# New priority offsets for the planner that orders every engine of a one-core backbone step

## The chip, the core and the metric

The kernel runs on one core of one Trainium2 chip. Its time is the device time of one execution in microseconds (us), the median of the runs shown. The core has a matrix engine (TensorE, PE in the profile, with its weight loads as PEld), a vector engine (VectorE, DVE), a scalar engine (ScalarE, ACT), GpSimd (POOL) and a sync engine (SyncE, SP). Each works through a list of instructions of its own, in order; SP and POOL also issue the transfers (DMA).

## The reference, cut to what matters

One inference step of a diffusion backbone with one layer: 1024 latent tokens and 128 context tokens, width 1024, all in float32.

```python
def block(x, mod, s_hgrn, s_rwkv, ffn_conv_fn, p):
    shift1, scale1, gate1, shift2, scale2, gate2 = jnp.split(mod[:, None, :], 6, axis=-1)
    h = rmsnorm(x, p['norm_mix_w']) * (1 + scale1) + shift1
    u = h @ p['w_in']
    o_a, s_hgrn_new = hgrn2_mixer(u[..., :P_A], p['lb'], p['hgrn_norm_w'], s_hgrn)
    o_b, s_rwkv_new = rwkv7_mixer(u[..., P_A:], p, s_rwkv)
    x = x + gate1 * (jnp.concatenate([o_a, o_b], axis=-1) @ p['w_out'])
    h = rmsnorm(x, p['norm_ffn_w']) * (1 + scale2) + shift2
    gt = ffn_conv_fn(h @ p['ffn_w_gate']) + p['ffn_conv_b']
    x = x + gate2 * ((jax.nn.gelu(gt) * (h @ p['ffn_w_up'])) @ p['ffn_w_down'])
    return x, s_hgrn_new, s_rwkv_new
```

`mod` is a projection of the conditioning vector (`ada_w`, 1024 by 6144). `hgrn2_mixer` is a gated linear recurrence with 4 heads of 128, run forward and backward; `rwkv7_mixer` is a delta-rule recurrence with 8 heads of 64, run forward and backward; the FFN (2816 wide) has a 3x3 depthwise convolution on its gate branch. The context runs through the same block, a final norm follows, and the context's final states are returned too.

## The kernel before, in words

The kernel doesn't write its instructions in the order in which they run. `step_kernel` walks through the computation once and records every operation with a class `Plan`: what it reads and writes, on which engine it may run, and the source function that asked for it, its kind (for instance `chains`, `weights`, `product`). `Plan.schedule` then lays all operations out in time with estimated durations: whenever an engine is free, it takes the ready operation of the highest rank. `Plan.issue` emits them in that order, so each engine's list is fixed when the kernel is built. Semaphores then hold an instruction until what it needs is there; an engine never goes past an instruction that waits.

The rank is the longest remaining path behind the operation (`tail`) plus a `lead`, both in us of the planner's own estimates, with some corrections for the matrix engine's modes and the activation tables:

```python
op.place, op.dense, op.lead, op.kind = None, False, self.lead + LEADS.get(self.kind, 0.0) + self.nudge(self.kind), self.kind
...
        i = self.seen[kind] = self.seen.get(kind, -1) + 1
        x = NUDGE.get(kind, ())
        return x[i // 16] if i // 16 < len(x) else 0
...
                r = op.tail + op.lead
...
            x = max(cand, key=rank)
```

`NUDGE` has a list of offsets for each kind: the first holds for the first 16 operations of that kind in the order of recording, the second for the next 16, and so on, each between -200 and 200. An operation that may go to several engines (most copies to ACT or DVE, most stores to POOL or SP) goes to the one whose turn comes first, so a rank can also decide its engine. A tile of on-chip memory gets its place when its first operation is laid out.

In the order of time, the kernel's stages are these.

- Up to about 75 us: nine blocks of rows of x are loaded, normed and transposed (`turned`, L1208), the first third of `ada_w` is multiplied by the conditioning vector (`mod_columns`, L1252 and L1257), and the modulated rows are split into a high and a low float32r part (`hh`, `hl`).
- Up to about 500 us: the input projection. Each block of 128 columns of `w_in` is loaded (`wr`), split into `wh` and `wl`, and multiplied in three passes (`proj`, L1139 to L1141). `conv_rkv` and `features` make the RWKV operands (`pk`, L1474), `elim` inverts small triangular systems (L1539, L1541), `hgrn_in` (L1302) makes the HGRN2 operands (its transposes are L1315); all go to DRAM (`d_ak`, `d_kb`, `d_v`, `d_hq` and so on).
- About 500 to 960 us: two chains of 18 RWKV steps each (`chains`, L1808), with `hgrn_block`, `hgrn_out`, `bonus_rows` and the rest of `ada_w` (`ada_block`, L1031, matmuls at L1046) between them. A step loads `kb` (L1771) and `W` (L1773, from `d_ak`), then the values from `d_v`; `prep` multiplies the first two (L1790), and four small groups of matmuls follow (L1837, L1844, L1852, L1861 and L1863). `W` has one buffer for each of the two chains.
- About 900 to 1061 us: the output projection by blocks of 128 rows (`wo_tile`, L2033 to L2035), each after `post` has loaded `d_y` (L1937), normed it and transposed it (L1957), then transposes of the FFN's input (L2047).
- About 1037 to 1545 us: the FFN's gate and up projections, in 22 tiles of 128 columns. `weights` (L2102) loads quarters of the weights, two of them by accumulating transfers on POOL's queue, and `pair` splits them (L2115); `product` (L2137, matmuls at L2145) multiplies; `ffn_mid` does the convolution on DVE (L2234). `down_sums` (L2249) prepares sums of the down projection's weights with accumulating transfers into `d_t`.
- About 1545 us to the end: the down projection (`three`, L2310), with the last norm and the stores.

Of the kernel before, what the change touches and what calls it, by code (L numbers as in the profile page):

```python
# [44 lines left out]
HUNGRY = 2.04  # L45
BUSY = 168.59
ADDS = 2.1
NUDGE = {'step_kernel': [-74, -18, -9, 150, 12, -123, -45, 8, -171, -78, -136, -179, 107, -143, -58, 0, -130, -65, -5, 128, 32], 'const': [-22], 'turned': [97, -42, -193, -76, -114], 'param_loads': [-72, -193], 'params': [-93, -75], 'first_columns': [18, -146, -118, -43], 'mod_columns': [-171, 58, -11, -11], 'modulated': [79, 153, 129, 10, 26], 'conv_rkv': [-39, -180, -157, 76, -193, 38, -43, -113, -6, -198, -181, -15, -22, 19, -60, 38, 0, -14, -4, -2, -12, -36, -52, -68, -4, -22, -7, 16, 98], 'features': [11, 15, 5, 7, 7, 4, 12, 18, 19, 13, 4, -13, -25, 2, -15, -18, 15, 1, -1, 8, 135, 22, 13, -7, -9, 49, -12, 10, 52, -6, -13, 149, 113, -14, -42, 40, -39, 200, 53, 147, 194, 162, 146, 69, 156, 106, 12, 157, 6], 'hgrn_in': [-21, 125, -9, -10, -3, -22, 47, 74, -1, 110, 113, 101, 77, 73, 55, 34, 25, 33, 38, 3, -25, 85, 74, 33, -51, -81, 69, -27, -33, -47, -41, -43, -40, -39, 0, -60, -47, 104, -54, -124, -85, -102, -45, -44, -41, -135], 'elim': [-31, 11, 4, -66, 30, -24, -2, -54, 26, -8, 14, -1, -80, -6, 0, 9, 118, 94, 159, 130, -37, 65, 67, 117, 163, 18, -87, 0, 0, 123, -122, 147, 145], 'chains': [147, 1, 46, 57, 14, 65, 0, -12, 8, 8, 11, 13, -3, -1, -1, 8, 67, -31, 7, 6, 1, 3, -22, 31, 4, -52, 20, 12, 26, 5, 58, 9, 0, 2, 61, -1, 16, 119, 137, 172, 177, 46, 70, 24, 16, 4, -11, -33, -33], 'prep': [72, -66, -26, 76, -2, 6, 0, -48, -40, 7, -15, -126, 100, -34, -86, 10], 'bonus_rows': [-177, -200, 51, -33, -72, -25], 'ada_block': [-6, 0, -21, 2, 10, 48, 37, 5], 'hgrn_block': [-12, -21, 0, -11, -8, -40, -96, -124, -53, -1, 72, 69, 5, 18, -5, -20, -19, -3, 2, 200, 3, 8, -46, -18, -44, -41, -3, -19, -22, 30, -20, -4, 0, 0, -13, 1, 60, 55, 95, 184, -18, 10, 6, 62, 89, -33, 1, 26, 2, 81, 128, 59, -7], 'hgrn_out': [9, -29, 34, 20, -53, 0, 0, -4, -64, 73, -70, 6, 3, 17, 75], 'mod_scale': [-188], 'wo_tile': [74, -16, -30, 7, -28, -29, 44, -7, 150, 73, 184, 90, 92, 97, 131, 0, -123, 77, 96, 48, 9, 28], 'post': [-28, -2, 151, -25, 41, 199, 67, 74, 86], 'stored': [62], 'put': [126, 0, 132, 32, 194], 'made': [111, 72], 'weights': [-144, 9, -60, 11, 102, -11, -130, -37, -192, 175, 155], 'pair': [133, -65, 41, -35, 1, -6, -22, -48, -174, -122, -112, 86, 10, 2, -49, 4, -81, 8, -141, -112], 'product': [70, 200, 104, 27, 29, -16, -16, -184, -68, -45, -132, -1, -164, -66, 41, 99, 16, -86, -25, -3, -14, -152, -70, -36, -54, -54, -93, 1, -120, -6, -172, -200, -200, -186, -91, -200, -200, -200, -200, -126, -200, -146, -155, 0, -4, 141, -88, -81, -17, -88, 127, 198, -96, -15, 92, -90, -194, -157, -102, 45, -194, -107, -185, -153, -160, 0, -26, -195, -33, -76, 56, -171, -19, -134, -23, -47, -50], 'save': [80, 75, 47, -69, -200, -35, -175, -91, -12], 'front': [-40, 75, -32, -36, -46, -20, -166, -162, 5, 15, -150, -134, -86, -150], 'ffn_mid': [-11, -35, -68, -65, -37, -17, -131, -39, -113, -200, -152, -200, -173, -60, -61, -92, -181, -170, -125, -98, -94, -42, -41, -6], 'down_sums': [-86, -18, -200, 128, 29, 15], 'rows_of_context': [12, -134], 'tokens': [-1, -10, -25, -182, -89], 'part': [6, -6, -2, -5, -5, -75, -113, -24, -27, 32, 111, 198, 153, 116, 3, 5, -41, -72, 105, -10, -77, -95], 'weight': [175, 0, 196], 'three': [-41, 113, 9, 55, -48, -18, 9, -30, -23, 25, -93, 0, -67, -24, -19, -60, -81, 0, 88, 128, -28, -21, -38], 'gate_row': [75], 'kept': [-40], 'gated': [-59, -47, 14, 62], 'normed': [-200, 0, -37], 'put_out': [-72, -6], 'total': [-53, 29, 69]}
LEADS = {'ada_block': 46.4, 'bonus_rows': 27.8, 'chains': -35.7, 'const': 113.0, 'conv_rkv': 0.0, 'down_weights': -36.2, 'elim': -4.6, 'features': 0.0, 'ffn_down': 14.5, 'ffn_mid': -1.7, 'finish': 52.5, 'finish_last': -12.3, 'first_columns': -38.6, 'front': 0.0, 'gate_row': 0.0, 'hgrn_block': -3.6, 'hgrn_in': 0.0, 'hgrn_out': 113.5, 'late': -0.7, 'made': 3.5, 'mod_columns': -1.2, 'mod_scale': 70.4, 'modulated': -24.2, 'pair': 8.2, 'param_loads': 9.6, 'params': -96.8, 'post': 3.0, 'prep': 119.5, 'product': -3.4, 'put': 0.0, 'save': 4.8, 'step_kernel': -1.0, 'stored': 0.0, 'three': -10.1, 'total': -0.3, 'turned': 4.0, 'weights': 0.0, 'wo_tile': 5.1}


# [126 lines left out]
class Plan:  # L178
# [213 lines left out]
    def nudge(self, kind):  # L392
# [4 lines that stand above are left out]
# [2086 lines left out]
```

## Time and profile before

| | |
|---|---|
| Median of 3 runs | 1804.65 us (1803.7 to 1806.81) |
| The profiled execution's own time | 1804.31 us |
| Its span, first to last instruction | 1802.5 us |
| Mean granted clock of TensorE | 0.990 |
| Instructions | 44849 |
| Moved by DMA | 352.98 MB, on the mean 196 GB/s |

In the lines of the profile, an engine's time is followed by its share of the span and the number of its instructions; a line such as L2145 is the line of the kernel that asked for the operation. A wait is written as the engine, tile and line that waited, then what ended the wait ("issue" where the profile shows nothing that did). Matmuls overlap each other, so a busy PE has work in flight and may still be slowed. PEclk is the share of TensorE's full clock that was granted. The chain of waits is followed back from the last instruction.

### The profile page before, as it was taken

How to read it: one execution, taken by the hardware profiler on the slowest of the kernel's cores; microseconds unless marked ns; L12 is line 12 of the kernel's file. 1: busy time of each engine (PE TensorE's matmuls, PEld its weight loads, DVE VectorE, ACT ScalarE, POOL GpSimd, SP SyncE). 2: the span in 40 equal slices, each digit the busy share in tenths (PEclk: the TensorE clock that was granted, in tenths of full speed). 3: DMA queues.
4: the chain of work that ended last, by engine and by line, in shares of the span. 5: the costliest groups of instructions: out<-in, count | busy, mean ns of one | idle time of the engine just before them, and what ended most of it. 6: DMA issues, size and time to landing. Idle time of an engine off the chain costs nothing.

```text
span 1802.5 us, 44849 instructions
## 1 busy us (share of the span) xinstructions
PE 1731.0 (96%) x17726; PEld 1551.9 (86%) x17726; DVE 1455.2 (81%) x2793; ACT 936.1 (52%) x1921; POOL 441.7 (25%) x701
## 2 busy tenths in 40 slices
PE   6999999999999999999998989999999999999998
PEld 4888888888978788887777889999999999788886
DVE  7558998977778878886868877998879889868875
ACT  6556756542256545663635754444444444665542
POOL 2114335353322222223211112233332323100000
PEclk9999999999999999999999999999999999999999
DMA  9226547486676668888967657688877767997674
GB/s 325 95 64 173 127 122 177 109 216 188 199 211 205 203 207 280 280 273 263 320 185 258 227 117 146 128 184 169 161 151 154 158 143 164 282 341 230 195 254 146
DMA packets 321930, 352.98 MB, mean 196 GB/s; under 512 B 67771, under 2 KB 240217, under 8 KB 321368
## 3 DMA queue, kind: packets, MB, share of 16 engines
q1 hardware_dynamic: 255528, 245.56, 45.7%
q0 software_dynamic: 66192, 104.57, 25.1%
q8 instruction: 139, 2.28, 0.5%
q14 instruction: 71, 0.58, 0.1%
HBM read 254.99 MB, written 118.10 MB: 207 GB/s over the span
## 4 chain that ended last, share of the span: by engine, by line
PE 82%; DVE 7%; DMA 6%; issue 2%; ACT 2%; SPq 0%; POOL 0%; DVEq 0%; POOLq 0%; ACTq 0%
PE banks L2145 25%; PE banks L2310 14%; PE banks L1139 7%; PE banks L1141 6%; PE banks L1140 6%; PE banks L1790 2%; DMA fx<-d_y 1%; PE banks L2033 1%; PE banks L2034 1%; PE banks L2035 1%; PE banks L1837 1%; PE banks L1659 1%; PE banks L1844 1%; PE banks L1861 1%; DMA d_kb<-top 1%
## 5 line engine op out<-in xcount | busy, mean ns | idle before, releaser
L1139 PE MATMUL banks<-hh,wh 128*128 128x384 f32 x768 | 282.0, 367 | 1.4 <-DVE fx L1327 1.4
L1140 PE MATMUL banks<-hl,wh 128*128 128x384 f32 x768 | 259.9, 338 | 0.0
L1141 PE MATMUL banks<-hh,wl 128*128 128x384 f32 x768 | 259.9, 338 | 0.0
L2234 DVE SCALAR_TENSOR_TENSOR low<-low,pf 128x1024 f32<-128x1024 f32 x176 | 225.0, 1280 | 9.5 <-ACT low L2228 6.9
L2145 PE MATMUL banks<-qm,wh 128*128 128x320 f32 x968 | 224.8, 312 | 2.6 <-ACT wh L2115 2.4
L2145 PE MATMUL banks<-qm,wl 128*128 128x320 f32 x528 | 164.1, 311 | 2.9 <-DVE wl L2115 2.9
L2145 PE MATMUL banks<-hbm,wh 128*128 128x256 f32 x880 | 164.1, 284 | 2.0 <-DVE low L2013 1.5
L2145 PEld LDWEIGHTS banks<-qm,wh 128*128 128x128 f32 x968 | 162.0, 190 | 3.3 <-ACT wh L2115 2.7
L1139 PEld LDWEIGHTS banks<-hh,wh 128*128 128x128 f32 x768 | 146.0, 190 | 21.7 <-issue 13.4
L1140 PEld LDWEIGHTS banks<-hl,wh 128*128 128x128 f32 x768 | 146.5, 191 | 2.1 <-issue 1.4
L1141 PEld LDWEIGHTS banks<-hh,wl 128*128 128x128 f32 x768 | 146.0, 190 | 0.0
L2145 PEld LDWEIGHTS banks<-hbm,wh 128*128 128x128 f32 x880 | 139.8, 191 | 3.2 <-DVE low L2013 1.8
L2145 PE MATMUL banks<-ham,wh 128*128 128x256 f32 (+1 forms) x616 | 131.7, 294 | 0.0
L2183 ACT COPY fx<-banks 128x256 f32<-128x256 f32 (+1 forms) x132 | 52.3, 398 | 143.5 <-PE banks L2145 142.4
L2145 PE MATMUL banks<-hbm,wl 128*128 128x256 f32 x440 | 124.8, 284 | 0.0
L2145 PEld LDWEIGHTS banks<-qm,wl 128*128 128x128 f32 x528 | 99.7, 189 | 4.2 <-DVE wl L2115 4.2
L2145 PEld LDWEIGHTS banks<-ham,wh 128*128 128x128 f32 x616 | 102.0, 190 | 0.1
L2115 ACT CAST wh<-low 128x512 fp32r<-128x512 f32 x88 | 54.4, 619 | 57.7 <-DMA low<-in_ffn_w_up_dram 32.4
L2145 PEld LDWEIGHTS banks<-hbm,wl 128*128 128x128 f32 x440 | 84.3, 192 | 0.0
L2145 PE MATMUL banks<-ham,wl 128*128 128x256 f32 (+1 forms) x264 | 77.1, 292 | 0.0
L2115 DVE TENSOR_TENSOR wl<-low,wh 128x512 fp32r<-128x512 f32 x88 | 60.3, 687 | 16.5 <-ACT wh L2115 16.1
L2254 POOL DMA_DIRECT2D d_t<-in_ffn_w_down_dram x44 | 43.0, 1093 | 86.5 <-DMA d_t<-d_t 42.2
(604 smaller groups left out, 4442.9 us busy)
## 6 DMA issues: line engine op xcount, KB each, us to landing
wr<-in_w_in_dram SPq DMA_DIRECT2D x34, 512.0 KB, 4.1
d_t<-in_ffn_w_down_dram POOLq DMA_DIRECT2D x57, 256.0 KB, 5.4
low<-d_a SPq DMA_DIRECT2D x54, 256.0 KB, 4.7
low<-d_ak SPq DMA_DIRECT2D x64, 192.0 KB, 4.4
low<-in_ffn_w_gate_dram SPq DMA_DIRECT2D x44, 256.0 KB, 3.5
low<-in_ffn_w_up_dram POOLq DMA_DIRECT2D x44, 256.0 KB, 5.5
low<-d_kb SPq DMA_DIRECT2D x36, 256.0 KB, 3.9
d_a<-low POOLq DMA_DIRECT2D x16, 576.0 KB, 4.4
```

The costliest lines, as they stand in the source:

```text
L1139: mm(o, wh[:, kt, :], hh[:, kt, c], kt == 0, False)
L1140: mm(o, wh[:, kt, :], hl[:, kt, c], False, False)
L1141: mm(o, wl[:, kt, :], hh[:, kt, c], False, kt == KT - 1)
L1659: mm(pv[r, i, :], xs[:, t0:t0 + 32], view(qy, t0, [[2 * m, 16 // m], [B + m, 2], [1, m]]), True, True)
L1790: mm(pa[h][:, P * w:P * w + P], kb[hc[h], w, :], W[hc[h], A0[h] + 192 * w:A0[h] + 192 * w + P], True, True)
L1837: mm(R[hc[h], 64 * w:64 * w + 64], av(h, w, 0), X[h][:, 0, w], True, True)
L2115: split(*w, src)
L2145: pe.matmul(o, a[:, kt, :], b[:, kt, :], start=start and first, stop=last, skip_group_check=not start)
L2183: act.copy(keep[n], y[:, 0:w])
L2234: dve.scalar_tensor_tensor(av, shifted(dy, dx), tap(3 * dy + dx), av, MUL, ADD)
L2254: acc(td[j][k], b)
L2310: pe.matmul(o, x, y, start=fresh and f, stop=l, skip_group_check=not fresh)
```

## The change

`NUDGE` gets new values; nothing else in the kernel is touched. The new values come from a search that judged each order over replays with random durations and random lateness of the transfers. 618 offsets stand in both versions; 9 are the same, and 274 differ by more than 50. Two kinds have one offset more than before (`weight` and `gated`). How far the offsets of a kind differ, as the median of the absolute differences: `ada_block` 8, `chains` and `hgrn_block` 12, `hgrn_in` 22, `prep` 26, `features` 30, `pair` 36, `conv_rkv` 38, `elim` 48, `three` 67, `ffn_mid` 68, `product` 98, `turned` 100, `down_sums` 134, `weights` 136. The leads (`LEADS`), the costs, the buffers and the operations stay as they are.

Nine of the 42 kinds, with the start of the longest list:

```diff
-'hgrn_in': [-21, 125, -9, -10, -3, -22, 47, 74, -1, 110, 113, 101, 77, 73, 55, 34, 25, 33, 38, 3, -25, 85, 74, 33, -51, -81, 69, -27, -33, -47, -41, -43, -40, -39, 0, -60, -47, 104, -54, -124, -85, -102, -45, -44, -41, -135],
+'hgrn_in': [-38, 41, -10, -9, -4, -40, -6, 65, 16, 167, 157, 136, 29, 21, 50, 30, -3, 3, 39, 5, 70, 11, 10, -19, -11, -16, -2, 19, -8, -14, -25, -37, -36, -37, -25, -62, -36, 154, -52, -90, -82, -96, -30, -38, -41, -30],
-'chains': [147, 1, 46, 57, 14, 65, 0, -12, 8, 8, 11, 13, -3, -1, -1, 8, 67, -31, 7, 6, 1, 3, -22, 31, 4, -52, 20, 12, 26, 5, 58, 9, 0, 2, 61, -1, 16, 119, 137, 172, 177, 46, 70, 24, 16, 4, -11, -33, -33],
+'chains': [-12, 7, 58, 70, 29, 57, 1, -9, -1, -10, 16, 18, 0, 0, 0, 4, 77, -53, 16, 8, 3, 30, -18, 35, 32, -33, 115, -29, 18, 40, 129, 1, -4, -10, 90, 82, 83, 76, 73, 184, 142, 17, 51, 4, 4, -8, -27, -45, 7],
-'prep': [72, -66, -26, 76, -2, 6, 0, -48, -40, 7, -15, -126, 100, -34, -86, 10],
+'prep': [49, -75, 0, 82, 43, 31, 99, -43, 1, 33, -8, -70, 33, 4, -101, -13],
-'ada_block': [-6, 0, -21, 2, 10, 48, 37, 5],
+'ada_block': [22, 5, -21, 0, 29, 23, 26, -1],
-'post': [-28, -2, 151, -25, 41, 199, 67, 74, 86],
+'post': [-28, -39, 124, -84, 61, 182, 99, 91, 98],
-'weights': [-144, 9, -60, 11, 102, -11, -130, -37, -192, 175, 155],
+'weights': [43, -44, 92, 147, 0, 8, -8, -18, 5, -12, -25],
-'pair': [133, -65, 41, -35, 1, -6, -22, -48, -174, -122, -112, 86, 10, 2, -49, 4, -81, 8, -141, -112],
+'pair': [136, -34, 76, -16, 38, 4, 105, 37, -22, 7, -52, 10, 19, 14, -44, -32, -22, 5, -84, -73],
-'product': [70, 200, 104, 27, 29, -16, -16, -184, -68, -45, -132, -1, -164, -66, 41, 99, 16, -86, -25, -3, -14, -152, -70, -36, ...],
+'product': [57, 177, 42, 46, 40, 20, 5, -5, 140, 121, 38, 192, -114, 25, 53, 97, 54, 40, 49, 185, 179, 184, 178, 64, ...],
-'down_sums': [-86, -18, -200, 128, 29, 15],
+'down_sums': [-199, -96, 3, 17, -130, -141],
```

More of the change, by code (lines that the diff above doesn't have):

```diff
@@ new lines @@
+NUDGE = {'step_kernel': [-1, 21, 23, 153, 19, -118, 24, 0, 59, 53, 38, -46, 7, -86, -57, -200, -162, -34, -65, 27, -37], 'const': [-1], 'turned': [45, 73, 123, 24, -81], 'param_loads': [-52, -27], 'params': [30, 141], 'first_columns': [-17, 0, 65, 95], 'mod_columns': [-200, 49, -70, -62], 'modulated': [34, -122, 14, -97, -13], 'conv_rkv': [-20, 28, 17, 14, -71, 21, 7, 6, 7, -131, -59, 65, -34, 2, -24, -4, -58, -28, -9, -11, -21, 2, -23, -64, -4, -36, -50, 143, 184], 'features': [6, -9, -1, 3, -13, 173, 166, 184, 184, 200, 149, -20, -36, 7, -27, -39, -22, -14, -14, -15, -12, -8, -18, -9, -17, 82, -12, 36, 109, 0, -7, 18, 92, -2, -53, -32, -50, 170, 95, 183, 157, 182, 192, 192, 196, 200, 169, 125, 124], 'hgrn_in': [-38, 41, -10, -9, -4, -40, -6, 65, 16, 167, 157, 136, 29, 21, 50, 30, -3, 3, 39, 5, 70, 11, 10, -19, -11, -16, -2, 19, -8, -14, -25, -37, -36, -37, -25, -62, -36, 154, -52, -90, -82, -96, -30, -38, -41, -30], 'elim': [17, 87, 0, -32, 20, -28, -25, -4, 80, -14, 86, 4, -1, -24, -14, 125, 199, 146, 179, 149, 76, 38, 74, 27, -3, -39, 69, 52, 13, -2, -7, 191, 129], 'chains': [-12, 7, 58, 70, 29, 57, 1, -9, -1, -10, 16, 18, 0, 0, 0, 4, 77, -53, 16, 8, 3, 30, -18, 35, 32, -33, 115, -29, 18, 40, 129, 1, -4, -10, 90, 82, 83, 76, 73, 184, 142, 17, 51, 4, 4, -8, -27, -45, 7], 'prep': [49, -75, 0, 82, 43, 31, 99, -43, 1, 33, -8, -70, 33, 4, -101, -13], 'bonus_rows': [49, -35, -103, -31, -186, -64], 'ada_block': [22, 5, -21, 0, 29, 23, 26, -1], 'hgrn_block': [31, -19, 139, -23, -94, -50, -93, -134, -96, 62, 82, 78, -23, 4, 4, -19, -18, -26, 49, 152, 4, 8, -95, -27, -41, -25, 87, 42, -65, 27, -3, 1, 1, -7, -23, 13, 61, 142, 176, 187, -16, 16, 9, 84, 186, 25, 34, 45, 8, 90, 104, 54, 12], 'hgrn_out': [8, -12, -31, -29, -73, -7, 20, 37, 0, 0, -66, 42, -18, 184, 5], 'mod_scale': [-188], 'wo_tile': [132, -14, -52, -13, -77, -45, 20, 14, 138, 89, 184, 105, 112, 117, 153, -46, 13, 104, 153, 65, -75, -18], 'post': [-28, -39, 124, -84, 61, 182, 99, 91, 98], 'stored': [164], 'put': [140, 90, 106, -49, -44], 'made': [131, -57], 'weights': [43, -44, 92, 147, 0, 8, -8, -18, 5, -12, -25], 'pair': [136, -34, 76, -16, 38, 4, 105, 37, -22, 7, -52, 10, 19, 14, -44, -32, -22, 5, -84, -73], 'product': [57, 177, 42, 46, 40, 20, 5, -5, 140, 121, 38, 192, -114, 25, 53, 97, 54, 40, 49, 185, 179, 184, 178, 64, 29, 32, 149, -6, 103, -18, -10, 4, -3, -2, 7, 12, -12, -55, -74, -88, 2, 2, -67, 65, 177, 23, 4, 22, 27, 36, 30, 41, 29, 17, 18, -12, 3, -18, -25, -52, -68, -48, -48, -31, 55, 41, 21, -34, -36, -36, -40, -56, -12, -27, -91, 8, -65], 'save': [105, 108, 53, 55, 13, 120, 47, 53, -164], 'front': [-17, -5, -19, 21, 73, 183, -1, -45, -50, 40, -69, 12, -29, -153], 'ffn_mid': [17, 31, -149, -11, 18, -24, 58, 51, 21, -13, 12, -149, -127, -154, -22, 26, -32, -74, -118, -29, -29, -24, -71, -200], 'down_sums': [-199, -96, 3, 17, -130, -141], 'rows_of_context': [-128, -42], 'tokens': [-35, -200, -165, -57, 82], 'part': [0, -36, -65, 9, 57, 17, -87, -74, -146, -145, -30, -154, -32, -28, -32, -63, -90, -146, 34, 112, -141, 13], 'weight': [0, 144, 90, 47], 'three': [-92, -24, -50, 1, 34, -59, -24, -5, -112, -198, -194, -193, -26, -159, -162, 89, -9, 200, 91, 195, -48, -47, -45], 'gate_row': [-16], 'kept': [-48], 'gated': [-101, -117, 49, 200, 19], 'normed': [-200, 181, -22], 'put_out': [-155, -71], 'total': [-200, -13, -29]}
```

1 line of the change is left out of this document (removed).

## The prediction

> **What bounds the kernel now.** I read the page's first three parts, then the stages in the view of windows, then TensorE's (PE's) waits, then the clock. The page comes first.
>
> ```profile
> span 1802.5 us, 44849 instructions
> PE 1731.0 (96%) x17726; PEld 1551.9 (86%) x17726; DVE 1455.2 (81%) x2793; ACT 936.1 (52%) x1921; POOL 441.7 (25%) x701
> q8 instruction: 139, 2.28, 0.5%
> ```
>
> PE has work in flight for 1731.0 of 1802.5 us, and the change alters none of its 17726 matmuls. An order can therefore move only the 71.5 us in which PE is idle, the time at a lower clock, and the small losses between short matmuls. Where the idle time lies is told by the windows, which I set at the borders of the stages (columns: stretch, length, then busy time and instructions of each engine, granted clock, DMA share, GB/s).
>
> ```profile
> 0.00:17.00 17.00, 3.43 (x16) 2.44 (x16) 6.93 (x27) 12.38 (x26) 11.88 (x33) 1.00 0.84 309
> 17.00:75.00 58.00, 57.10 (x409) 47.43 (x410) 44.65 (x115) 37.57 (x77) 0.95 (x8) 1.00 0.65 199
> 75.00:300.00 225.00, 223.82 (x2348) 195.97 (x2347) 178.41 (x343) 137.13 (x277) 73.18 (x134) 1.00 0.50 129
> 300.00:500.00 200.00, 191.76 (x2092) 176.60 (x2090) 162.54 (x350) 84.84 (x164) 80.48 (x141) 0.98 0.66 180
> 500.00:960.00 460.00, 434.95 (x7692) 371.64 (x7692) 368.45 (x884) 255.67 (x583) 109.95 (x204) 0.99 0.81 244
> 960.00:1061.00 101.00, 91.59 (x475) 77.08 (x474) 81.57 (x152) 64.79 (x142) 12.70 (x18) 0.95 0.63 207
> 1061.00:1518.00 457.00, 456.62 (x3424) 455.51 (x3423) 392.04 (x569) 201.32 (x393) 137.28 (x143) 1.00 0.75 154
> 1518.00:1555.00 37.00, 32.41 (x217) 30.05 (x216) 33.77 (x49) 23.27 (x42) 6.87 (x8) 1.00 0.88 261
> 1555.00:1790.00 235.00, 235.00 (x1038) 191.72 (x1037) 180.95 (x296) 116.19 (x214) 8.42 (x14) 1.00 0.75 242
> 1790.00:1802.50 12.50, 4.32 (x30) 3.50 (x29) 5.89 (x16) 2.94 (x9) 0.00 (x0) 0.86 0.22 85
> ```
>
> PE's idle time, as length less busy time, is 13.6 us at the start, 0.9, 1.2, then 8.2 (end of the projections), 25.1 (the two RWKV chains with the HGRN2 work), 9.4 (output projection), 0.4 (FFN), 4.6 (change to the down projection), 0.0 and 8.2 (tail). The FFN and the down projection, 692 us together, have nothing to give and can only lose. The places with something to give hold 8.2 + 25.1 + 9.4 + 4.6 = 47.3 us. Who ends PE's waits there (engine, line, releaser; us in total, times, longest):
>
> ```profile
> PE banks L1852 <- issue: 6.0, 3, 3.6
> PE banks L1315 <- DVE fx L1327: 3.2, 1, 3.2
> PE banks L1790 <- DMA low<-d_ak: 2.9, 5, 1.1
> PE banks L2145 <- DVE wl L2115: 2.9, 4, 2.3
> PE banks L1046 <- DMA fx<-in_ada_w_dram: 2.8, 1, 2.8
> PE banks L1957 <- DVE fx L1953: 2.7, 1, 2.7
> PE banks L2145 <- ACT wh L2115: 2.4, 1, 2.4
> PE banks L1837 <- DMA low<-d_v: 1.4, 2, 1.2
> ```
>
> These eight rows sum to 24.3 us. Four name a transfer, or an issue that the profile doesn't see. For three others the chain of waits shows a transfer one or two steps further back:
>
> ```profile
> 406.47 3.29 issue
> 409.77 2.30 DMA d_hq<-fx
> 959.18 9.11 DMA fx<-d_y
> 1035.17 7.26 DMA low<-in_ffn_w_up_dram
> ```
>
> PE's 3.2 us at L1315 follow a DVE stage held up by POOL's issue of a store and its landing; its 2.7 us at L1957 follow the load of d_y (9.11 us), and its 2.4 us at L2115's weights the load of the up weights (7.26 us). So most of the 24.3 us is work that came late by a transfer, and the other 23.0 of the 47.3 us are gaps behind short dependencies.
>
> The second loss is the clock. The granted clock is 0.50 in nine stretches of 3.41 us ahead of the tail. Here are the first and last of the nine with their sum row, the mean of the stretches just ahead of them, and the FFN's matmuls at half and full clock.
>
> ```profile
> 320.98:324.39 3.41, 3.40 (x11) 3.40 (x12) 3.28 (x9) 3.37 (x4) 3.41 (x6) 0.50 0.98 266
> 1054.84:1058.26 3.42, 3.28 (x15) 3.01 (x16) 3.33 (x6) 3.20 (x8) 0.00 (x0) 0.50 0.00 0
> sum 30.72, PE 30.57 PEld 27.86 DVE 23.86 ACT 18.21 POOL 9.41; mean PE 3.40 PEld 3.10 DVE 2.65 ACT 2.02 POOL 1.05
> sum 30.69, PE 14.68 PEld 11.25 DVE 16.32 ACT 16.30 POOL 6.41; mean PE 1.63 PEld 1.25 DVE 1.81 ACT 1.81 POOL 0.71
> 1039.64 0.46 PE L2145 MATMUL banks<-qm,wh 128*128 128x320 f32 x2
> 1040.08 0.46 PE L2145 MATMUL banks<-qm,wh 128*128 128x320 f32 x2
> 1045.31 0.74 PE L2145 MATMUL banks<-qm,wh 128*128 128x320 f32 x2
> 1046.10 0.74 PE L2145 MATMUL banks<-qm,wh 128*128 128x320 f32 x2
> ```
>
> Three such matmuls take 0.44 us (1039.64 to 1040.08) and 0.79 us at half clock (1045.31 to 1046.10). A half-clock stretch full of wide matmuls thus loses about 3.41 / 2 = 1.7 us, and the nine at most 15.4. Ahead of each PE was busy 1.63 us of 3.41 on the mean: the half clock follows a stall, so the same stall is paid twice.
>
> **The change part by part.** It replaces the priority offsets that a planner adds to each operation, in groups of 16 of a kind. No operation, shape, byte or buffer changes: matmuls, DVE and ACT work and DMA sizes cost 0 more or less. A store that either POOL or SP may issue can change its queue. The changed part is only when each is issued, so I cost it by stage.
>
> (1) Start, 14.5 us idle up to 75 us. DMA is at 0.84 share with 309 GB/s while nine row blocks arrive, and PE has nothing else. I take 0; the bounds are -2.8 and +2.8, one stall of the ada_w kind either way.
>
> (2) 75 to 300 us, the dense stages and the tail: -1.2 and -0.4 are all that could be gained in the first two, 0 in the down projection. The tail's 8.2 us is one chain of norm and store. I take 0, and put the FFN's loss among the rivals.
>
> (3) Chain loads, 6.0 + 2.9 + 1.4 = 10.3 us. W has one buffer per chain group, so no order can start its load ahead of the last matmul that reads it; the sync queue (SP) shows this, and the load behind it lands 4.4 us later:
>
> ```profile
> SPq L1771 <- PE banks L1790: 27.2, 14, 6.6
> SPq L1773 <- PE banks L1863: 26.5, 17, 8.8
> low<-d_ak SPq DMA_DIRECT2D x64, 192.0 KB, 4.4
> 695.25 0.34 PE L1852 MATMUL banks<-low 128*64 128x64 f32 x4 [2.08 <-issue]
> ```
>
> An order can only put other PE work there. The last row stops twelve matmuls into a group of sixteen, for nothing that the profile shows; since the instructions come by DMA too (the q8 row of the page: 139 packets, 2.28 MB), I estimate that they were late. Between 0 and 10.3 us I take a quarter, -2.6, because the buffer, not the rank, decides.
>
> (4) The other late work, 3.2 + 2.9 + 2.8 + 2.7 + 2.4 = 14.0 us. These have spare buffers or can have PE work placed over them, and a load ranked earlier would have them ready. Between 0 and -14.0 I take half, -7.0.
>
> (5) Clock. Six half-clock stretches follow the stalls of (3) and (4), three each. A quarter of 3 x 1.7 and a half of 3 x 1.7 is -1.3 and -2.6.
>
> (6) New stalls. An order that ranks some loads earlier puts others later: the same SP and POOL queues carry them, and DMA is 0.81 busy in the chain stage. What is late next is whatever stands behind a moved load on SP, a chain's kb load or an ada_w block above all. The trace can't show them; the bounds are 0 and the size of what (3) to (5) give, 13.5. I charge three of half the size of a stall of (4) (14.0 / 5 / 2 = 1.4) and one half-clock stretch: 3 x 1.4 + 1.7 = +5.9, nearest to the row of the 2.9 us in five pieces.
>
> (7) The 23.0 us of short gaps, PE's changes between narrow and wide matmuls, and stores that go from POOL to SP or back. An order shuffles these; I take 0, bounds -6 and +6, a quarter of the 23.0.
>
> Sum: -2.6 - 7.0 - 1.3 - 2.6 + 5.9 = -7.6 us. The profiled execution took 1804.31 us, 1.8 more than its span; the median of the runs is 1804.65, so they agree to 0.34. 1804.31 - 7.6 = 1796.7; I forecast 1797, with a range of its own from 1786 to 1801.
>
> **The Trainium skill on the clock.** Its page "TensorE: Matmul & The Clock Gate", section "HAM oscillation — how this bites in real kernels", says that an idle gap of more than about 3.4 us is what brings the clock down. The trace differs: ahead of the nine half-clock stretches PE was busy 14.68 of 30.69 us, so shorter stalls suffice here. By the page only the longest wait (3.6 us, in term 3) costs clock, and the sum would be -2.6 - 7.0 - 0.4 + 4.2 = -5.8, or 1798.5; I keep the rows.
>
> **The rivals.**
>
> A, nothing gained: the stalls change place, (6) takes all of the 13.5, and the time is 1804. For it: eight waits of 1.4 to 6.0 us spread over 700 us, none dominant, and a single buffer behind 10.3 of the 24.3. Against it: 14.0 us where rank does decide.
>
> B, slower: the FFN loses its cover. Between 1061 and 1518 us PE idles 0.4 us, but DVE is busy 392 of 457 (86%) and SP waits long for the weights' transfers to add up:
>
> ```profile
> SPq L2121 <- DMA low<-in_ffn_w_up_dram: 110.4, 19, 9.0
> ```
>
> Each pair of weights passes load, accumulating load, cast and subtraction ahead of its product, over four buffers. The offsets of these kinds are among those that change most (medians of 136 for the weights and 98 for the products, against 12 for the chains). If the order lets the next tile's weights stand behind the gate's convolution on DVE, PE waits as at 1043 us: 2.4 us and 1.7 us of clock, 4.1 each. Two of these over 22 tiles eat the -7.6, and the third decides: 1804.3 - 7.6 + 12.3 = 1809, which is the case's time; five make 1817. Against it: the stage runs at 0.4 us idle today with offsets just as far apart.
>
> C, much better: all of the 24.3 us are hidden and six half-clock stretches go (10.2 us), 1804.3 - 34.5 = 1770; with half of the new stalls, as in (6), 1773 to 1780.
>
> **How the numbers follow.** Forecast 0.44, A 0.20, B 0.26, C 0.10. Changes of less than 0.2% (3.6 us) can't be told from none. Forecast and C are faster (0.54), A is the same (0.20), B slower (0.26). For the range, the part of B beyond 1813 (0.1) and most of C under 1783 (0.08) are left out: 1783 to 1813.
>
> **What would show it.** In the windows, PE's idle time from 300 to 1061 us falls from 42.7 to some 35 us, the half-clock stretches from nine to seven or fewer, the FFN and down projection keep at most 0.5 us idle, and the start and tail keep 13 to 15 and 8 us. The wait of L1790 for d_ak stays near 2.9 us, while the waits of L1046, L1957 and L1315 shrink. The prediction is wrong if PE's idle time in the FFN is over 5 us (B), if the chains' stage alone gains over 12 us (its short gaps, then, were worth more than the late transfers), or if the start moves by over 3 us.

## The result, and the profile after

The changed kernel takes 1794.31 us (median of 6 runs, 1789.29 to 1798.28) against 1804.37 us for the kernel before on the same chip (6 runs, 1803.61 to 1807.44). The ratio is 0.9941 with a 95% interval of 0.9923 to 0.9959. In a second session (six more runs of it) the median was 1797.70 us against 1805.92, the ratio 0.9953 (0.9938 to 0.9968). So the gain is real, 8.2 to 10.1 us by the medians, and near the 7.6 forecast. What the profile tells of where it came from is another matter.

The changed kernel's page, then its windows at the same borders (same columns as before). Its profiled execution took 1795.13 us.

```profile
span 1793.4 us, 44872 instructions
PE 1727.2 (96%) x17726; PEld 1548.7 (86%) x17726; DVE 1459.4 (81%) x2799; ACT 932.5 (52%) x1907; POOL 444.0 (25%) x708
```

```profile
0.00:17.00 17.00, 3.42 (x16) 2.44 (x16) 6.40 (x26) 12.29 (x25) 11.63 (x33) 1.00 0.82 304
17.00:75.00 58.00, 56.42 (x407) 46.61 (x408) 44.54 (x115) 37.34 (x77) 1.05 (x8) 1.00 0.66 201
300.00:500.00 200.00, 193.25 (x2169) 178.14 (x2164) 165.62 (x354) 86.24 (x171) 81.15 (x146) 0.99 0.68 185
500.00:960.00 460.00, 435.89 (x7688) 370.98 (x7689) 369.71 (x891) 249.66 (x568) 115.17 (x209) 0.99 0.80 243
960.00:1061.00 101.00, 94.88 (x514) 80.64 (x513) 86.17 (x160) 66.90 (x145) 12.71 (x18) 0.97 0.66 213
1061.00:1518.00 457.00, 456.93 (x3433) 456.50 (x3432) 396.14 (x572) 205.93 (x394) 140.06 (x146) 1.00 0.76 157
1518.00:1555.00 37.00, 35.73 (x212) 32.24 (x211) 34.87 (x49) 21.71 (x39) 6.32 (x8) 1.00 0.91 256
```

PE idles 13.6 us at the start as before, 37.0 us from 300 to 1061 us (42.7 before), 0.1 us in the FFN (0.4) and 1.3 us in the change to the down projection (4.6). The clock of the output projection's window rose from 0.95 to 0.97: ahead of the tail the half clock now holds for 20.5 us, six stretches instead of nine; in two of the rows below, two of them follow each other (same columns).

```profile
323.77:327.18 3.41, 3.41 (x11) 3.41 (x12) 3.28 (x9) 3.37 (x4) 3.41 (x6) 0.50 0.96 255
630.97:637.79 6.82, 5.65 (x93) 5.14 (x94) 1.96 (x4) 3.10 (x8) 0.54 (x1) 0.50 0.97 287
883.55:886.97 3.42, 3.42 (x18) 3.20 (x16) 3.29 (x8) 0.20 (x1) 0.00 (x0) 0.50 1.02 207
1047.39:1054.22 6.83, 5.31 (x24) 4.84 (x23) 5.87 (x12) 6.14 (x13) 0.00 (x0) 0.50 0.01 2
```

Waits of PE in the whole run, those on which the next sections rest (same columns as before):

```profile
PE banks L1852 <- issue: 5.2, 2, 4.0
PE banks L1474 <- DVE top L1465: 3.9, 3, 3.1
PE banks L1790 <- DMA low<-d_ak: 3.0, 5, 1.3
PE banks L1474 <- DVE top L1466: 2.4, 2, 1.2
PE banks L1046 <- DMA top<-in_ada_w_dram: 1.6, 1, 1.6
PE banks L1790 <- ACT g1m L2007: 1.5, 1, 1.5
PE banks L1315 <- DVE fx L1327: 1.3, 1, 1.3
PE banks L2145 <- DVE low L2204: 1.3, 1, 1.3
PE banks L1957 <- DVE fx L1953: 1.2, 1, 1.2
PE banks L2145 <- ACT wh L2115: 0.3, 1, 0.3
```

Fixed windows deceive here, because a faster order has other work in the same stretch (514 matmuls against 475 from 960 to 1061 us). So I worked out a work curve from each trace. Every matmul is weighted by the mean interval from start to start of its form (line and shape) in the trace of before; at each border of the stretches (in us of before's profiled execution) I looked up when another execution had issued the same sum of work. The table gives, for each stretch, the us by which it was longer (+) or shorter (-) than in before's profiled execution. The curve ends at 1795 us, just ahead of the last products.

| Execution | 0–75 | 75–300 | 300–500 | 500–950 | 950–1075 | 1075–1525 | 1525–1560 | 1560–1775 | 1775–1795 |
|---|---|---|---|---|---|---|---|---|---|
| after | 0.6 | 2.9 | -3.5 | 0.1 | **-5.3** | -0.6 | **-4.3** | -0.2 | -0.9 |
| after, run again (e4) | -0.1 | 3.6 | -2.3 | 2.6 | **-5.7** | -0.6 | **-4.3** | -0.2 | -0.9 |
| before, run again (e8) | 0.3 | 3.8 | -4.3 | 2.6 | 0.0 | 0.0 | -0.9 | 0.0 | 0.0 |

Up to 950 us the gain of the new order is nothing (0.6 + 2.9 - 3.5 + 0.1 = +0.1). Two borders hold what is left: the change from the output projection to the FFN (-5.3, "first border" below) and the change from the FFN to the down projection (-4.3, "second border"). The nine columns sum to -11.3, while the execution is 9.2 us shorter. The other 2 us go behind the end of the curve: in the new order the half clock of the tail begins while the last products still run (1784.7 us; before, 1798.9, 3 us after PE's last product). Before and after, three of these products behind the same short wait:

```profile
1793.61 0.63 PE L2310 MATMUL banks<-qm,hbm 128*128 128x256 f32 x3 [0.65 <-ACT banks L2441]
```

```profile
1784.67 1.01 PE L2310 MATMUL banks<-qm 128*128 128x256 f32 x3 [0.65 <-ACT banks L2441]
```

**What changed at the first border.** Timelines of POOL and PE, before first, then after (columns: start, duration, operation, and in brackets the idle time before it and what ended it):

```profile
1032.93 0.53 POOL L2056 DMA_DIRECT2D d_h<-low  x1 [15.44 <-DMA low<-d_h]
1035.17 1.35 POOL L2120 DMA_DIRECT2D low<-in_ffn_w_up_dram  x1 [1.71 <-DVE wl L2115]
1043.12 0.56 PE L2145 MATMUL banks<-qm,wh 128*128 128x320 f32 x2 [2.45 <-ACT wh L2115]
```

```profile
1030.87 0.53 POOL L2056 DMA_DIRECT2D d_h<-low  x1 [16.05 <-ACT low L2013]
1031.45 1.34 POOL L2120 DMA_DIRECT2D low<-in_ffn_w_up_dram  x1
1039.06 0.56 PE L2145 MATMUL banks<-qm,wh 128*128 128x320 f32 x2 [0.31 <-ACT wh L2115]
```

Before, the accumulating load of the FFN's first weights (L2120) is issued 1.71 us after POOL is free, because DVE gets to the split at L2115 late; the load lands late, and PE waits 2.45 us behind ACT's cast. After, DVE does that split at 1030.43 instead of 1032.96, the load goes out behind the store at once, 3.6 us ahead of the FFN's first product instead of 1.8, and the wait is 0.31 us. The load itself was also shorter: 4.9 us to its landing, where the chain before has 7.26. PE's wait at L1957 fell there too (2.7 to 1.2).

**What changed at the second border.** PE and DVE before, with a load and a cast of the down projection's weights, then PE and DVE after:

```profile
1533.68 0.42 PE L2145 MATMUL banks<-qm,wl 128*128 128x320 f32 x1 [2.30 <-DVE wl L2115]
1547.77 1.42 PE L2310 MATMUL banks<-qm 128*128 128x512 f32 x5 [1.68 <-ACT low L2202]
1527.78 5.24 DVE L2234 SCALAR_TENSOR_TENSOR low<-low,pf 128x1024 f32<-128x1024 f32 x4
1532.93 0.69 DVE L2115 TENSOR_TENSOR wl<-low,wh 128x512 fp32r<-128x512 f32 x1
1539.66 7.14 DMA low<-in_ffn_w_down_dram
1546.83 0.62 ACT L2292 CAST qm<-low 128x512 fp32r<-128x512 f32 x1 [1.15 <-DMA low<-in_ffn_w_down_dram]
```

```profile
1525.91 0.56 PE L2145 MATMUL banks<-qm,wh 128*128 128x320 f32 x2 [1.27 <-DVE low L2204]
1535.59 2.91 PE L2310 MATMUL banks<-qm 128*128 128x512 f32 x12
1538.33 0.46 PE L2145 MATMUL banks<-ham,wh 128*128 128x320 f32 x2
1516.25 9.21 DVE L2234 SCALAR_TENSOR_TENSOR low<-low,pf 128x1024 f32<-128x1024 f32 x7
1525.77 0.68 DVE L2115 TENSOR_TENSOR wl<-low,wh 128x512 fp32r<-128x512 f32 x1
```

Before, four taps of the convolution (L2234) stand ahead of a split of weights on DVE, and PE waits 2.30 us for it. The 1.68 us at L2310 end with ACT's copy of an FFN result out of its accumulator bank (L2202). That copy stands on ACT behind the cast at L2292, which waited 1.15 us for a load of 7.14 us. After, seven taps stand ahead of such a split (1525.8), and PE's one wait there is 1.27 us, for an FFN result that DVE takes out of its bank (L2204). The down projection then starts at 1535.6 (1543.9 before). The FFN's last product is at 1567.1 (1555.1 before): 123 down products now stand ahead of it, 27 before. So the 2.30 us have no transfer behind them, while the 1.68 us have one two steps back.

### The profile page after: what moved, and what is told of

It reads as the page before. It is cut to its first block, busy times and chain, and to the rows that moved or that the text cites. A ratio compares the mean times of both kernels' runs of the same rounds, so it can differ in the third digit from the quotient of the medians.

```text
span 1793.4 us, 44872 instructions
## 1 busy us (share of the span) xinstructions
PE 1727.2 (96%) x17726; PEld 1548.7 (86%) x17726; DVE 1459.4 (81%) x2799; ACT 932.5 (52%) x1907; POOL 444.0 (25%) x708
## 5 line engine op out<-in xcount | busy, mean ns | idle before, releaser
L2234 DVE SCALAR_TENSOR_TENSOR low<-low,pf 128x1024 f32<-128x1024 f32 x176 | 225.2, 1281 | 12.2 <-ACT low L2228 9.7
L2183 ACT COPY fx<-banks 128x320 f32<-128x320 f32 (+1 forms) x132 | 52.4, 398 | 111.6 <-PE banks L2145 111.6
L2115 ACT CAST wh<-low 128x512 fp32r<-128x512 f32 x88 | 54.4, 619 | 65.8 <-DMA low<-in_ffn_w_up_dram 42.5
L2115 DVE TENSOR_TENSOR wl<-low,wh 128x512 fp32r<-128x512 f32 x88 | 60.3, 687 | 9.9 <-ACT wh L2115 9.5
L2115 ACT CAST wh<-wr 128x512 fp32r<-128x512 f32 x66 | 39.8, 621 | 47.8 <-PE banks L2145 27.6
```

What stands on the lines that cost most here:

```text
L2115: split(*w, src)
L2183: act.copy(keep[n], y[:, 0:w])
L2234: dve.scalar_tensor_tensor(av, shifted(dy, dx), tap(3 * dy + dx), av, MUL, ADD)
```

## The experiments

The theories. Theory 1: the gain is made where the work curve has it, at the borders, by the order of the stages there. Theory 2: the gain is tolerance, as the search's random lateness of transfers would suggest; an order that bears late transfers better should win more the later they come. Further rivals stand in the expectations. In them "old" and "new" are the offsets of before and after. All medians are set against the kernel before in the same session (its medians lie within 1804 to 1806 us; e1 to e4, e5 to e8 and e9 to e12 are three sessions, each on a chip of its own).

**The late stages alone (e1_late_new).** Before, with new offsets for all kinds from the output projection to the end:

```diff
-'post': [-28, -2, 151, ...], 'weights': [-144, 9, -60, ...], 'three': [-41, 113, ...], ...
+'post': [-28, -39, 124, ...], 'weights': [43, -44, 92, ...], 'three': [-92, -24, ...], ...
```

> The old offsets for all kinds of the first stages, the new ones for the kinds of the output projection, the FFN and the down projection: TensorE's order is that of the kernel before up to about 860 us and that of the changed one later. Theory 1 (the gain is made at two borders between stages, 5.6 us between 950 and 1050 us and 4.3 us between 1525 and 1550 us; nothing of it before): 1794 to 1797 us, the whole gain. Theory 2 (the gain comes from better covered late transfers and fewer half-clock stretches everywhere, four of which went before 860 us): half of it stays away, 1799 to 1801 us. Theory 3 (any reshuffling moves the time by some us either way): no forecast.

1805.24 us; ratio 0.9994 (0.9977 to 1.0011): no gain. The work curve has -4.3 at the second border, but +3.0 at the first. There PE has new waits (window 940 to 1080 us):

```profile
PE banks L2047 <- ACT low L2013: 4.8, 2, 2.8
PE banks L2145 <- ACT qm L2075: 3.1, 1, 3.1
PE banks L2145 <- DVE qm L2075: 1.8, 1, 1.8
```

Theory 1 in this form fell: the late offsets by themselves don't bring the first border's gain.

**FFN and down projection alone (e2_ffndown_new).** As e1, with the output projection's kinds (`wo_tile`, `post`, `stored`, `put`, `made` and their part of `step_kernel`) old as well.

> The new offsets only for the kinds of the FFN and the down projection: TensorE's order is that of the kernel before up to about 1048 us. Theory 1: only the second border gains, 4.3 us, 1800 us. Theory 2: these two stages had 0.4 and 0.0 us idle, 1803 to 1805 us.

1800.38 us; 0.9966 (0.9949 to 0.9983). The work curve has -0.5 at the first border and -4.3 at the second, where the waits are those of after. The second border is made by these offsets alone.

**The down projection's offsets undone (e3_down_old).** After, with old offsets for its kinds:

```diff
-'three': [-92, -24, ...], 'total': [-200, -13, -29], 'rows_of_context': [-128, -42], ...
+'three': [-41, 113, ...], 'total': [-53, 29, 69], 'rows_of_context': [12, -134], ...
```

> The new offsets, but the old ones for the kinds of the down projection: TensorE's order is that of the changed kernel up to about 1515 us. Theory 1 with the second border's gain made by the down projection's own loads and splits: 4.3 us slower than the changed kernel, 1798 to 1799 us. Rival: that gain is made by the order in which the FFN's last tiles run, whatever comes behind: as the changed kernel, 1794 us.

1798.62 us; 0.9960 (0.9943 to 0.9978). The time is the one that Theory 1 gave here, but not for its reason: the border kept -3.8, and 2.2 us were lost within the down projection. So it is the FFN's order that makes the border, not the down projection's.

**The convolution's offsets undone (e12_fd_oldmid).** e2 with the old list of `ffn_mid`:

```diff
-'ffn_mid': [17, 31, -149, -11, ...],
+'ffn_mid': [-11, -35, -68, -65, ...],
```

> The new offsets for the FFN and the down projection as in the run that had only these, except that the convolution's kind keeps its old ones. Theory 1: the second border's 4.3 us hang on where VectorE runs the last convolutions against the splits, so they are lost: 1804 us. Rival: they hang on the products' own order: 1800 us.

1804.96 us; 0.9990 (0.9973 to 1.0008). The border is down to -1.6, and the FFN and the down projection lose 1.7 and 0.8. PE's waits from 1510 to 1560 us:

```profile
PE banks L2145 <- DVE low L2204: 1.5, 1, 1.5
PE banks L2310 <- DVE qm L2292: 0.8, 2, 0.5
PE banks L2310 <- DVE hbm L2292: 0.7, 1, 0.7
PE banks L2310 <- ACT qm L2292: 0.6, 1, 0.6
```

The convolution's place among the splits carries most of the second border (2.7 of 4.3 us): with its old offsets the down projection's operands (L2292) come late, and 90 down products stand ahead of the FFN's last one instead of 123.

**One DVE operation moved (e11_before_swap).** Before, with the split of weights that PE waited 2.30 us for two places further up on DVE, ahead of two of the four taps:

```diff
+        at = {op.id: i for i, op in enumerate(self.order)}
+        self.order.insert(at[8352], self.order.pop(at[8425]))
```

> The kernel before with one VectorE instruction two places up: in the FFN's last tile the split's subtraction (L2115, ahead of which PE waits 2.3 us at 1533 us) runs ahead of the last two convolution taps that stand before it. Theory 1 (the second border is a matter of VectorE's order there): 2.3 us less at that place, 1802 us. Rival: PE only comes to its next wait earlier (L2310, 1.7 us, behind a load of 7.1 us), 1804 us.

1809.35 us; 1.0011 (0.9990 to 1.0032): no gain. The wait went elsewhere (PE, line numbers shifted by 2):

```profile
1534.45 0.56 PE L2147 MATMUL banks<-qm,wh 128*128 128x320 f32 x2 [2.06 <-DVE low L2206]
1548.33 1.88 PE L2312 MATMUL banks<-qm 128*128 128x512 f32 x7 [1.09 <-ACT low L2204]
```

What the moved split had held up (2.30) is now paid, as 2.06 us, for the next operation on DVE that takes an FFN result out of its bank (L2204 of before, here L2206). So here a wait taken from one product came up at the next; of the orders that were run, only the interleaving of the new FFN offsets removed most of it.

**The output projection's offsets undone (e5_outp_old).** After, with old lists for those kinds:

```diff
-'wo_tile': [132, -14, -52, ...], 'post': [-28, -39, 124, ...], ...
+'wo_tile': [74, -16, -30, ...], 'post': [-28, -2, 151, ...], ...
```

> The new offsets, but the old ones for the kinds of the output projection: TensorE's order is that of the changed kernel up to about 857 us, the rest has the new offsets for the FFN and the down projection. Theory 1a (the first border's 5.5 us come from the new offsets of the output projection, fitted to what the chains' stage leaves over): they are lost, and the time is 1800 to 1804 us. Theory 1b (they come from the earlier stages' new order): they stay, 1795 us.

1818.1 us; 1.0071 (1.0043 to 1.0099): slower than either kernel. PE's waits from 940 to 1090 us, the largest two:

```profile
PE banks L1957 <- DVE fx L1953: 6.0, 2, 5.6
PE banks L2047 <- ACT low L2041: 4.4, 2, 2.7
```

With e1, e2 and after, all with the new FFN, this is a square for the first border: early offsets old, output projection old -0.5 (e2); old, new +3.0 (e1); new, old +13.7 (e5); new, new -5.3 and -5.7 (after and e4). The two sets pay only together. The early stages' offsets, which gain nothing up to 950 us, leave the work in another state there, and the output projection's are fitted to it. Theory 1a had the direction but not the size (1800 to 1804 us); neither set of offsets holds the border by itself.

**The wait of the first border by itself (e9_before_noacc, e10_after_noacc).** In before and after, the first FFN tile's accumulating load goes to a spare place in DRAM as a plain copy, so these two kernels leave one sum out:

```diff
+                    if op.id == self.first_sum:
+                        a, k = (self.spare, a[1]), {}
```

> The kernel before in its own order, but the first tile's accumulating load (the up weights onto the gate weights) goes to an unused place in DRAM: that one sum is left out, and nobody waits for its landing. Theory 1 (the first border's gain is this load: issued 1.8 us ahead of the FFN's first product before, 3.8 us ahead after the change): PE's wait of 2.4 us at L2145 for the weights' split and the half-clock stretch behind it go, 4 us less, 1800 to 1801 us. Rival: the waits behind it (L2047 for the modulation, 2.1 us, L2145 for low L2013, 1.5 us) grow by as much, 1804 us.

> The changed kernel with the same one load sent elsewhere. Theory 1: it waits 0.3 us for it, so no difference to the changed kernel beyond 0.5 us (1795 to 1797 us), and the kernel before without that wait comes to within 2 us of it at the first border. Rival: as in the kernel before without it, 4 us less.

In the order of before: 1802.44 us; 0.9979 (0.9964 to 0.9995), 3.1 us less than the 1805.5 beside it (the interval is 0.9 to 6.5 us). The wait is the one of after (line numbers shifted by 2 to 4):

```profile
1040.85 0.56 PE L2149 MATMUL banks<-qm,wh 128*128 128x320 f32 x2 [0.31 <-ACT wh L2117]
```

The border's gain in the work curve is -1.9. This alone would not settle it, since e11, whose order up to 1530 us is that of before, has -2.7 there. But in e11 too the wait is gone: its load was issued as late as before (1.8 us ahead of the FFN's first product), yet landed after 5.0 us (second row below).

```profile
1038.02 1.35 POOL L2122 DMA_DIRECT2D low<-in_ffn_w_up_dram  x1 [1.71 <-DVE wl L2117]
DMA to landing us min/median/max: 5.0/5.0/5.0
1043.84 0.56 PE L2147 MATMUL banks<-qm,wh 128*128 128x320 f32 x2 [0.32 <-ACT wh L2117]
```

In the other profiles of the old order that load took 6.6 to 7.3 us (before, e8, e2, e12) and PE waited 1.8 to 2.45 us; in the new order (after, e4, e3) it took 4.9. So the late issue makes the wait only together with a long load; why the load is shorter in one execution than in another isn't shown. Cut finer, the work curve gives the first border in three parts (us against before's profiled execution, as in the table above):

| Execution, order at this border | 950–1036 | 1036–1044 | 1044–1075 |
|---|---|---|---|
| e8, old | 1.2 | -0.2 | -1.0 |
| e2, old | 1.0 | -0.6 | -0.9 |
| e12, old | 0.4 | -0.2 | 0.0 |
| e11, old, wait gone by itself | 1.0 | -2.1 | -1.5 |
| e9, old, load sent elsewhere | 1.7 | -2.1 | -1.5 |
| after, new | -2.0 | -2.1 | -1.2 |
| e4, new | -2.4 | -2.1 | -1.2 |
| e3, new | -1.9 | -2.1 | -0.4 |
| e10, new, load sent elsewhere | -3.9 | -2.1 | -1.5 |

The wait is worth 2.1 us wherever it is gone (3.1 by the medians of e9). About 2 us more are gained ahead of it, in the output projection itself: a half-clock stretch stands there in five of the six profiles of the old order (not in e12) and in none of the four of the new. Which operation's place does that isn't shown. The last part isn't the new order's, since most profiles of the old order have it too. In after without the load: 1793.16 us; 0.9928 (0.9906 to 0.9949). Its interval overlaps those of after (0.9941 and 0.9953), and its wait of 0.3 us is unchanged, so the 2 us more at its border (-7.5) are not shown to come from the load.

**The same order again (e8_before_again, e4_after_again).**

> The kernel before as it is. Its times were 1799.6 to 1811.4 us in the last set of runs. Theory: the spread of one and the same order is made in the projections' and chains' stages, where TensorE waits on transfers and for nothing that the profile shows; a second profile differs from the first by up to 6 us there, and by under 1 us from 1075 us on. Rival: the spread is the same share of every stage (a clock that differs between executions).

> The changed kernel as it is, once more. Its six times were spread over 9 us (1789.3 to 1798.3), those of the kernel before over 3.8. Theory: the spread is in the chains' stage, where PE's long waits for nothing that the profile shows come and go between executions; the two borders' gains are in every execution. Then a second profile differs from the first by up to 6 us between 500 and 960 us and by less than 1 us in all other stages. Rival: the first border (two stalls behind transfers) comes and goes.

1804.08 us (0.9993, 0.9975 to 1.0011; runs from 1795.91 to 1808.93) and 1797.70 us (0.9953; runs from 1796.19 to 1801.28). The work curves, in the table above, differ from those of the same order by up to 4.3 us in a stretch ahead of 950 us, and by at most 0.9 in any stretch behind it. The spread isn't in the chains' stage alone: e8's two largest differences lie between 75 and 500 us. And the first border isn't the same in every execution: e11 differs there from before by 2.7 us in the same order, though all five profiles of the old order (0.2 to -2.7) stay above those of the new (-4.5 to -5.7). Seven executions whose orders are those of before up to 859 us (before, e8, e9, e11, e1, e2, e12) are 0, 2.4, -1.9, 1.9, -2.8, -5.6 and -5.9 at 950 us; five in the order of after, or with other lists only for later stages (after, e4, e3, e10, e5), are 0.1, 3.8, 4.1, -0.8 and -4.6. The means are -1.7 and +0.5: no gain by the new order ahead of 950 us that this spread lets one see.

**Late transfers (e6_before_traffic, e7_after_traffic).** Every eighth transfer on SP is followed by one of 512 KB from DRAM to DRAM that nobody waits for, 126 in all:

```diff
+                    if sent % 8 == 0:
+                        self.units["SP"].dma_start(self.extra[sent // 8 % 8], self.extra_from)
```

> The kernel before with 126 transfers more, one of 512 KB from one DRAM place to another behind every eighth transfer of the sync queue: nothing of it is used, it only makes the other transfers late. Theory 2 (the new order bears lateness of transfers better): before loses 10 to 30 us by it, and the changed kernel half of that or less. Theory 1 (the gain sits at two borders, where DVE and ACT order decides): both lose the same to 2 us.

> The changed kernel with the same 126 transfers. Theory 2: it is over 15 us faster than the kernel before with them. Theory 1: the difference stays 8 to 10 us.

1884.07 us in the order of before (1.0439, 1.0409 to 1.0468) and 1873.58 us in that of after (1.0365, 1.0331 to 1.0398). The difference is 10.5 us, against 8.2 to 10.1 without the traffic: by the medians before loses 79 us and the changed kernel 76 to 79. The chains' stage, where most transfers stand on the path, in e6 and e7 (columns of the windows):

```profile
500.00:950.00 450.00, 407.52 (x7264) 349.49 (x7259) 333.77 (x814) 230.15 (x521) 109.81 (x203) 0.96 0.88 276
```

```profile
500.00:950.00 450.00, 409.89 (x7280) 351.93 (x7283) 335.99 (x825) 225.12 (x514) 112.00 (x206) 0.96 0.87 276
```

Both idle 40 to 42 us in 450 us there, and by the work curve they lose 35.7 and 37.8 us. At the first border they stand at +5.3 and -4.9, at the second at +3.1 and -1.6. Theory 2 isn't borne out: as a whole the new order bears late transfers no better. At the first border its lead is larger than without the traffic (10.2 us instead of 5.3), in one profile of each; whether that is tolerance or spread isn't shown, as the runs of e7 reach from 1860.31 to 1875.83 us and the profiled one took 1865.71.

No mixture of old and new was faster than the changed kernel; e3's 1798.62 us beside 1797.70 in the same session can't be told from it.

## Why the prediction was right in its sum and wrong in its places

The forecast of 1797 stands beside 1794.3 and 1797.7. By its own steps:

- **(1) and (2), start, dense stages, tail, 0:** right. The start moved 0.6 us; 75 to 300 us shows +2.9, where the same old order shows +3.8. The tail gave 0.9 and lost 2 in its last products.
- **(3) Chain loads, -2.6:** the buffer decides, as argued: L1790's wait for `d_ak` is 3.0 (2.9). The wait for `d_v` is gone, but waits for nothing visible ("issue") between 500 and 950 us are 8.5 us, 5.2 of them at L1852. The prediction's estimate that late instructions make them holds (last section). The term was 0 in its stage.
- **(4) Other late work, -7.0 of 14.0:** the five rows fell from 14.0 to 4.6 (1.3 + 0.2 + 1.6 + 1.2 + 0.3), more than the half taken. But the step that failed is that a shorter wait is a shorter stage. L1315's and L1046's 3.1 us came back as other waits ahead of 950 us. Only the rows at the two borders were kept.
- **(5) Clock, -3.9:** fewer stretches, as forecast, in the profiles of the two kernels: nine and ten in two of the old order, six and seven in two of the new, some three at 1.7 us. But the order isn't shown to be the reason: up to 1060 us e2 and e12 have six and seven in the old order, and e3 has ten in the new. Of the three stretches fewer, two lie where the curve shows no gain; the one from 960 to 1061 us is part of the first border's 5.3.
- **(6) New stalls, +5.9:** their size was right, their place not. Three waits grew: L1474 behind L1465 (0.8 to 3.9) and L1466 (2.4), L1790 behind L2007 (1.5), 7.0 us more. None is behind a `kb` or `ada_w` load. L1474's is partly spread: the old order, run again, shows 2.3 behind L1465 instead of 0.8.
- **(7) Short gaps, 0, and the second border:** mis-sized. The change to the down projection had one row of (4) at half of 2.9 (-1.4) and its dense stage at 0; it gave -4.3, by more down products laid among the FFN's last ones (123 instead of 27 in after and e2, 138 in e3; in e12, with 90, it gave -1.6).

So ahead of 950 us what terms (3) to (6) stand for cancels, and the sum came out near because the borders gave 9.6 us, where the forecast had only parts of (4) and (5). That the number fits is in good part luck: terms that cancelled stood for a gain in places that the forecast had at little or nothing. The mechanism of (4), a load ranked in time, is shown for one place alone (L2120, by e9 and e11) at 2.1 us, and there the load's own duration counts as well as its rank.

**The rivals.** A's mechanism, stalls that change place, is what happened in the 875 us up to 950; it doesn't describe the borders. B didn't occur in after (FFN 0.07 us idle), but its kind, offsets that don't fit the neighbour's, is what e5 shows at the first border (+13.7). C is out. Of the signs named beforehand, idle time (37.0, some 35 forecast), stretches (six), FFN, start, L1790, L1046, L1957 and L1315 all came as forecast, yet L1046 and L1315 had no part in the gain that the curve shows: a wait that shrinks is no proof that its stage did. On the clock, the rows that the prediction kept to, by which shorter gaps suffice, are borne out: past the start, one single wait of PE after the change is over 3.4 us (4.0, at L1852), and there are still six half-clock stretches ahead of the tail. The tail's own begins at 1784.67 us, behind waits of 0.53, 0.52 and 0.65 us. The rule weighed in the prediction, 3.4 us of idle, is too strict for this kernel.

## What to carry to other kernels

In a kernel with fixed lists, compare two orders by when the same work is done, not by fixed windows or by waits that come and go: further profiles of the same order tell which stretches differ by more than chance. One more isn't enough: at the first border e8 repeated the order of before to 0.0 us, e11 was 2.7 us shorter. Offsets of neighbouring stages have to be judged together; the new order with one stage's offsets left old is 13 us slower than the old one. And moving one late operation up didn't help in the one place where it was tried, on a full engine, since an operation that it passed was awaited next.

## What the runs showed of the hardware that was not expected

The same instruction lists take 1798.1 to 1812.7 us within one session (29 runs of before), and the profiles place most of the spread ahead of 950 us, in the stages with small matmuls and DMA shares of 0.5 to 0.8.

PE's pauses with nothing visible to wait for ("issue") come to 8.0 us from 75 to 950 us in before, 7.9 in e8, 8.5 in after and 6.1 in e4, whatever the order. The traces show what holds PE there. All 24 such pauses of these four profiles stand a whole number of 256 instructions apart in PE's list, to one (matmuls, weight loads and PE's few semaphore instructions counted). Each ends 1.3 to 1.7 us after the end of a transfer of 16 KB on the queue that the profile calls "instruction" (q8: 139 packets, one for 255 of PE's 35452 matmuls and weight loads), and the packet's number goes with the number of the block. So PE waits there for the next block of its own list. An example from after: the packet ends at 630.71 us, and PE's longest pause, 628.17 to 632.14 us at L1852, ends 1.43 us later. What makes some of these packets late isn't shown.

The 126 extra transfers, 66 MB more beside 353, cost 76 to 79 us (by the medians) though nothing waits for them: the mean DMA share in the chains' stage only rose from 0.80 to 0.88, but the chains' loads of `d_ak` took 6.6 us to land in e6 instead of 5.1 in before (medians), and PE's waits for them between 500 and 950 us grew from 2.9 to 6.3 us.
